# Moving two token blocks' transfers and splits to other places, and one block product to another bank, in an encoder block on one core

## The chip, the cores and the metric

The kernel runs on one core of one Trainium2 chip. The metric is the device time of one execution in microseconds (us); lower is better. Each kernel is run several times and the median is given, with the lowest and the highest beside it. A profiled execution also gives a span: the time from the first to the last instruction in the trace. It is a little shorter than the execution's own time.

## The reference, cut to what matters

The kernel computes one encoder block in float32 with a batch of 1, 1024 tokens and a width of 1024. Three mixers run side by side on the same normalised input, each is gated and projected, the three are merged by sigmoid gates, and one output projection follows:

```python
h = rms_norm(x, g_pre[layer])
a_qkv, bq, bk, bv, mq, ga, gb, gm, mg = jnp.split(h @ w_in[layer], split_at, axis=-1)
...                                   # oa: dilated windows, ob: grouped queries, om: cross-attention
ya = (oa * jax.nn.silu(ga)) @ w_br_a[layer]
yb = (ob * jax.nn.silu(gb)) @ w_br_b[layer]
ym = (om * jax.nn.silu(gm)) @ w_br_m[layer]
gates = jax.nn.sigmoid((mg + b_merge[layer]).astype(jnp.float32)).astype(dt).reshape(b, s, N_BRANCHES, d)
merged = gates[:, :, 0] * ya + gates[:, :, 1] * yb + gates[:, :, 2] * ym
out = merged @ w_out[layer]
x = x + rms_norm(out, g_post[layer])
```

The change touches how the last part of `mg` is computed. `mg` has 3 x 1024 columns, that is 24 *units* of 128 columns. A unit is one product of a 1024 x 128 block of weights with the 1024 x 1024 input. In the kernel the rows of the result are the 128 columns of the weights, and the 1024 tokens run along the free axis.

## The kernel before, in words

**Numbers.** TensorE (PE) multiplies float32 values in three passes. Each operand is split into a high part, rounded to a shorter type (fp32r), and a low part, the rest. A product is then high x high + high x low + low x high. The helper `split` (lines 103 to 106) makes the two parts: ScalarE (ACT) copies the source into the high tile (line 105), then VectorE (DVE) subtracts the high part from the source and writes the low tile (line 106). The helper `passes` (lines 121 to 125) issues the matmuls of one product into one bank of the accumulator memory (PSUM). The input lies in SBUF as `hh0` to `hh7` (high) and `hl0` to `hl7` (low), each 128 x 1024, one for each block of 128 input channels.

**Banks.** PSUM has eight banks of 128 x 512. Two of them belong to the dense units for the whole kernel: `psd` (lines 61 and 62), which hands out a tile named `d`, two in turn. The other six are laid out anew for each stage by `phase_psum` (line 67). In the stage of the pairs they are a ring of six single banks (`pss1`, tiles named `s`), and in the stage of the branch projections three tiles of two banks each (`pss`, tiles named `sc`).

**Stages.** In order of time: the memory branch and the keys of the grouped-query branch, woven into dense units; the grouped-query attention; two stages of block products for values and keys; the dilated attention (twelve items, four groups of heads by three dilations), woven into the last dense units (`weave`, line 176); the *pairs*; the branch projections; the output projection. PE's instructions stand in the order in which the program writes them in the whole kernel. In the dilated stage and in the pairs that order is also kept on ACT, DVE, GpSimd (POOL) and SyncE (SP), because a `manual_schedule` covers these engines there (lines 1601 and 1647). An instruction there never overtakes one that is written ahead of it on its engine. SP issues nearly all transfers from one queue, in order; a transfer whose target is still being read holds up all those behind it.

**The pairs** (lines 1642 to 1822). Two of the 24 units are computed earlier, and the other 22 form eleven pairs, n = 0 to 10. A pair is a product of two weight units (256 columns) with 1024 channels by 1024 tokens, seen as a 2 x 2 by 2 x 2 block matrix and computed by Winograd's scheme with seven block products in place of eight (`PRODUCTS`, line 1656): A11·B11, A12·B21, S2·T2, S3·T3, S4·B22, S1·T1, A22·T4. A is the weights, B the input, S1 to S4 are sums of weight blocks, and T1 to T4 sums of token blocks. One block product has 12 matmuls of 128 x 128 by 128 x 512 and fills one bank. In the last pair the order is another (`nth`, line 1675): A22·T4 is fifth, S4·B22 sixth and S1·T1 seventh.

The token sums T1 to T4 are computed once, early in the kernel, and lie in DRAM (`tsd`). Each consists of four tiles of 128 x 512, loaded raw by `load_block` (line 1584) into the low tile and then split in place by `split_block` (line 1589). T2 and T3 are loaded and split while the last item of the dilated attention runs. Of T1, tiles 0 and 1 are loaded there too (line 1463), and tiles 2 and 3 at the head of the pairs (line 1811). T4 goes into the upper token halves of `hh0` to `hh3` and `hl0` to `hl3` (line 1653), which nothing reads in the pairs but which the dense units read until the end of the dilated stage. It is loaded last of all (line 1813).

For each pair and each i from 0 to 6 the main loop (lines 1815 to 1822) writes the block product on PE (`prod`), the evacuation of the product before it (`evac`), and a *slot* of work for later (`slot`, line 1759):

- `evac` adds on DVE: intermediate results into tiles `sp` (line 1689), results into tiles `rs` (line 1689), which are then multiplied by the token's reciprocal norm `rb` (line 1695). ACT applies tanh to `rs` (line 1696) and sends it to DRAM.
- `block_of` splits a weight block or a weight sum (`sf`) into a tile `ch` of high and low halves (lines 105 and 106).
- `own_blocks` splits A11 and A12 of the next pair into `wh` and `wl`, 128 x 1024 each.
- `weight_sum` (line 1666) makes S1 to S4 on POOL from the weights `wr`. `load_pair` (line 1571) loads these, two tiles in turn.
- In pair 0 the slots 2, 3 and 4 also split T1 (two tiles each in slots 2 and 3) and T4 (all four in slot 4). In pairs 0 to 4 some slots hold a step of the dilated attention's last combination (`COM`).

After the pairs come 24 units of the branch projections (`y_unit`, two times 12 matmuls into one `sc` tile) with weights loaded into `wr` and split into halves of `wh` (`y_split`).

Of the kernel before, what the change touches and what calls it, by code (L numbers as in the profile page):

```python
# [9 lines left out]
R = mybir.dt.float32r  # L10
# [5 lines left out]
S = 1024  # L16
NT = 8
P = 128
# [32 lines left out]
def block(ctx: ExitStack, tc: tile.TileContext, x, xT, memT, cst, msk, bcst, tabA, gpost,  # L51
# [10 lines left out]
    def psd():  # L62
        return ps.tile([P, 512], F32, name="d", tag="d", bufs=2)
# [15 lines left out]
    def pss1():  # L79
        return bank["p"].tile([P, 512], F32, name="s1", tag="s1", bufs=bank["n"][1])  # L80
# [41 lines left out]
    def passes(out_ps, terms):  # L122
        n = len(terms)
        for i, (a, b) in enumerate(terms):
            PE.matmul(out_ps, a, b, start=i == 0, stop=i == n - 1)  # L125
# [117 lines left out]
    def pool(name, side="left"):  # L243
        p = tc.tile_pool(name=name, bufs=1, side=side, reuse_waits="tile")
        return p, p.__enter__()

    def close(p):
        p.__exit__(None, None, None)
# [605 lines left out]
    def slot():  # L854
        return vp.tile([P, 1024], R, name="sl", bufs=8)
# [257 lines left out]
    tbp, tb = pool("tb")  # L1113
    tab = [tb.tile([P, S], F32, name=f"tab{j}") for j in range(2)]
# [8 lines left out]
    for n in range(6):  # L1123
        for i, (an, bn) in enumerate(PRODUCTS):
            dst = pss1()
# [54 lines left out]
    with tc.tile_pool(name="aa", bufs=1, reuse_waits="tile") as aa:  # L1180
# [263 lines left out]
        def joined(*pieces):  # L1444
            pieces = [x for x in pieces if x]
            return (lambda: [fn() for fn, _ in pieces]), JOINED

        def plan(it, pre, nxt):

            out = []  # L1450

            def combining(T):
                while todo and T == STEP_T[-len(todo)]:
                    todo.pop(0)()

            def tokens(T):
                if T >= 2:
                    for nm, k in late[:2]:
                        split_block(nm, k)
                    del late[:2]  # L1460
                if T == 5:
                    token_tiles("T1", [ab.tile([P, S], R, name=f"a{c}", bufs=2) for c in "qk"])
                    load_block("T1", (0, 1))

            def keys(key, T):
                (k_fetch if T == 1 else k_add)(*key)

            def ready():
                if pre and pre["key"][1] == 2:
                    fetch, *steps = combine(pre["key"][0], [OG.pop((pre["key"][0], x)) for x in range(3)])  # L1470
                    fetch()
                    todo.extend(steps)

            if it and not pre:
                out.append(it["scores"][0])
            for T in range(NT if it else 4):
                if T == 2 and pre:
                    out.append(pre["stats"])
                if T < LAG:
                    if pre:  # L1480
                        out.append(pre["trans"][T + 8 - LAG])
                elif it:
                    out.append(it["trans"][T - LAG])
                if it:
                    out.append(it["soft"][T])
                out.append((lambda T=T: combining(T), 0.0))
                if it and not nxt:
                    out.append((lambda T=T: tokens(T), 0.0))
                if it and it["ahead"] and T in (1, 5):
                    out.append((lambda T=T: keys(it["ahead"], T), 0.0))  # L1490
                if T == 3:
                    out.append(joined(pre and pre["pv"][1], it and it["scores"][1]))
                    if it:
                        out.append(it["values"][1])
                    if pre and it:
                        out.append((ready, 0.0))
                if T == 7:
                    out.append(joined(it["pv"][0], nxt and nxt["scores"][0]))
                    if nxt:
                        out.append(nxt["values"][0])  # L1500
            return out
# [67 lines left out]
        def load_pair(n, u):  # L1569
            BL[n][u] = wp.tile([P, 1024], F32, name="wr", bufs=WR)  # L1570
            nc.sync.dma_start(BL[n][u], wu[U_M + pairs[n][u]])

        def own_blocks(n):
            wh = wp.tile([P, 1024], R, name="wh")
            wl = wp.tile([P, 1024], R, name="wl")
            split(wh, wl, BL[n][0])
            for j in range(2):
                BL[n][("A11", "A12")[j]] = wh[:, half[j]], wl[:, half[j]]
# [3 lines left out]
        def token_tiles(nm, tiles):  # L1582
            TB.setdefault(nm, []).extend([t[:, half[x]] for x in range(2)] for t in tiles)

        def load_block(nm, ks=range(4)):
            for k in ks:
                nc.sync.dma_start(TB[nm][k][1].bitcast(F32), tsd[int(nm[1]) - 1, k])

        def split_block(nm, k):
            h, l = TB[nm][k]  # L1590
            split(h, l, l.bitcast(F32))
# [26 lines left out]
        for n in range(len(seq)):  # L1618
# [5 lines left out]
            last = n + 1 == len(seq)  # L1624
# [24 lines left out]
    lo, hi = half  # L1649
    srp, sr = pool("sr")  # L1650
    SF = [sr.tile([P, 512], F32, name=f"sf{j}") for j in range(4)]
    token_tiles("T1", [tb.tile([P, S], R, name=f"T1{k}", tag=f"tab{k - 2}") for k in (2, 3)])
    TB["T4"] = [(hh[k][:, hi], hl[k][:, hi]) for k in range(4)]
    TB["B11"] = [(hh[k][:, lo], hl[k][:, lo]) for k in range(4)]
    TB["B21"] = [(hh[k + 4][:, lo], hl[k + 4][:, lo]) for k in range(4)]
# [2 lines left out]
    last = len(pairs) - 1  # L1658

    def part(n, j):  # L1660
        return BL[n][j // 2][:, half[j % 2]]

    def weight_sum(n, j):
        u, v, op = {1: (part(n, 2), part(n, 3), OP.add), 2: (SF[0], part(n, 0), OP.subtract),
                    3: (part(n, 0), part(n, 2), OP.subtract), 4: (part(n, 1), SF[1], OP.subtract)}[j]
        G.tensor_tensor(SF[j - 1], u, v, op=op)  # L1666

    def block_of(n, nm):
        src = part(n, 3) if nm == "A22" else SF[int(nm[1]) - 1]
        t = sr.tile([P, 2, 512], R, name="ch", bufs=5)  # L1670
        split(t[:, 0], t[:, 1], src)
        BL[n][nm] = t[:, 0], t[:, 1]

    def nth(n, i):

        return PRODUCTS[{4: 6, 5: 4, 6: 5}.get(i, i) if n == last else i]

    def prod(n, i):
        an, bn = nth(n, i)
        dst = pss1()  # L1680
        ah, al = [v.rearrange("p (k f) -> p k f", k=4) for v in BL[n][an]]
        passes(dst, [t for k in range(4) for t in (
            (ah[:, k], TB[bn][k][0]), (ah[:, k], TB[bn][k][1]), (al[:, k], TB[bn][k][0]))])
        return dst
# [46 lines left out]
    def g_mult(i, k):  # L1731
        if i != 1:
            ot, gt = GG[i, k]
            V.scalar_tensor_tensor(ot, ot, 0.5, gt, op0=OP.mult, op1=OP.mult)
# [24 lines left out]
    def slot(n, i):  # L1759

        first = n == 0
        if not first and i == 1 and n < last:
            load_pair(n + 1, 1)
        if i == 6 and n + 1 < last:
            load_pair(n + 2, 0)
        todo_ = (("S2",), ("S3", "A22"), ("S4",), ("S1",)) if first else (("A22",), ("S4",), ("S1",))
        for nm in todo_[i] if i < len(todo_) else ():
            block_of(n, nm)
        if first:
            for nm, k in {2: (("T1", 0), ("T1", 1)), 3: (("T1", 2), ("T1", 3)), 4: (("T4", 0), ("T4", 1), ("T4", 2), ("T4", 3))}.get(i, ()):  # L1770
                split_block(nm, k)
        if n < last:
            if i == 3:
                weight_sum(n + 1, 1)
                weight_sum(n + 1, 3)
                own_blocks(n + 1)
            elif i == 4:
                weight_sum(n + 1, 2)
                block_of(n + 1, "S3")
            elif i == 5:  # L1780
                weight_sum(n + 1, 4)
                block_of(n + 1, "S2")
        if (n, i) in COM:
            com[COM[n, i]]()
        if (n, i) == (5, 0):
            close(cbp)
            pre["pp"], pre["p"] = pool("pre", "right")
        k = n - (last - 4)
        if 0 <= k < 4:
            if i == 0:  # L1790
                g_load(2, k)
            elif i == 4:
                g_mult(2, k)
        if n == last:
            if i == 0:
                y_load(0)
                y_load(1)
            elif i in (3, 4):
                for k in range(2 * i - 6, 2 * i - 4):
                    g_split(2, k, lo)  # L1800
            elif i in (5, 6):
                for k in range(2 * i - 10, 2 * i - 8):
                    g_split(2, k, hi)
            if i == 2:
                y_split(0)
                y_load(2)

    for j in (1, 2, 3, 4):
        weight_sum(0, j)
    load_pair(1, 0)  # L1810
    load_block("T1", (2, 3))
    load_pair(1, 1)
    load_block("T4")
    before = None
    for n in range(len(pairs)):
        for i in range(7):
# [276 lines left out]
```

## Time and profile before

| what | value |
|---|---|
| time before, median of 3 runs | 1434.83 us (1433.94 to 1435.69) |
| profiled execution, its own time | 1434.1 us |
| span of that execution | 1432.3 us |
| PE busy | 1405.2 us (98% of the span) |
| PE's weight loads (PEld) busy | 1130.6 us (79%) |
| DVE busy | 993.7 us (69%) |
| ACT busy | 657.0 us (46%) |
| POOL busy | 509.9 us (36%) |
| granted TensorE clock, mean | 0.999 of full speed |
| HBM traffic over the span | 138 GB/s |

How to read the rows that follow. Times are in us from the start of the span. The page names an engine, a line of the kernel (L125 is line 125), an operation and the tiles that it writes and reads (`sc<-hh,wh` writes `sc` and reads `hh` and `wh`). In a timeline a row begins with its start and its duration; `x4` stands for four like instructions in a row, and a bracket gives the idle time just ahead of it on its engine and what ended that. The idle time of an engine that does not set the pace costs nothing. Matmuls are pipelined, so the durations of single matmuls overlap, and the distance between starts is the better measure. In the chain of waits the work that ended last is followed back to what released each step. SPq is SP's queue of transfers.

### The profile page before, as it was taken

The numbers are of one execution on the slowest core, as the hardware profiler recorded it, in microseconds if no ns is written. First come the engines' busy times: TensorE is split into PE (matmuls) and PEld (weight loads), VectorE is DVE, ScalarE is ACT, GpSimd is POOL, SyncE is SP. The second block draws the span as 40 slices with busy tenths as digits, with TensorE's granted clock in tenths as the row PEclk, the third lists the DMA queues.
The fourth block names the chain that finished last, engine by engine and source line by source line (L and its number), as shares of the span: only waits on it lengthen the run. The fifth ranks groups of instructions, "written<-read, shape, count | busy, mean of one in ns | idle before, by whom it ended". The sixth has DMA issues, their size and how long they took to land.

```text
span 1432.3 us, 21216 instructions
## 1 busy us (share of the span) xinstructions
PE 1405.2 (98%) x7556; PEld 1130.6 (79%) x7556; DVE 993.7 (69%) x1765; ACT 657.0 (46%) x1423; POOL 509.9 (36%) x390
## 2 busy tenths in 40 slices
PE   7999999999999999999999999999999999999998
PEld 7899986666666888888888878877787887888887
DVE  7765468777773785688776778755887787659643
ACT  6543356665555445322156666656433434213221
POOL 0415603666675001333143354411343330044222
PEclk9999999999999999999999999999999999999999
DMA  6332012222210879444553445364334454667122
GB/s 233 109 120 75 16 64 76 88 97 75 75 55 31 281 241 299 139 175 155 189 149 110 119 137 157 89 176 140 129 122 147 177 176 151 245 220 276 42 88 103
DMA packets 114138, 198.68 MB, mean 139 GB/s; under 512 B 24624, under 2 KB 55408, under 8 KB 114032
## 3 DMA queue, kind: packets, MB, share of 16 engines
q1 hardware_dynamic: 87824, 166.75, 36.4%
q10 hardware_dynamic: 26208, 30.58, 6.1%
q8 instruction: 59, 0.97, 0.3%
q14 instruction: 47, 0.39, 0.1%
HBM read 142.40 MB, written 54.89 MB: 138 GB/s over the span
## 4 chain that ended last, share of the span: by engine, by line
PE 82%; DVE 6%; ACT 4%; DMA 3%; issue 3%; POOL 2%; SPq 0%; ACTq 0%; POOLq 0%; DVEq 0%
PE s L125 19%; PE sc L125 9%; PE d L143 7%; PE d L147 6%; PE d L145 6%; PE s L1059 5%; PE sc L1939 5%; PE ov L761 4%; PE s L1343 2%; PE tr L1399 2%; PE s L745 2%; PE tr L727 2%; PE s L746 2%; PE d L542 2%; PE d L1059 1%
## 5 line engine op out<-in xcount | busy, mean ns | idle before, releaser
L143 PE MATMUL d<-hh,wh 128*128 128x512 f32 x480 | 194.8, 406 | 1.7 <-DVE fth L228 1.7
L145 PE MATMUL d<-hl,wh 128*128 128x512 f32 x480 | 194.4, 405 | 0.0
L147 PE MATMUL d<-hh,wl 128*128 128x512 f32 x480 | 190.5, 397 | 0.0
L752 POOL TENSOR_TENSOR bl<-bl,bp 128x512 f32<-128x512 f32 x96 | 131.4, 1369 | 53.6 <-ACT bp L748 48.1
L105 ACT ACTIVATE wh<-wr 128x512 fp32r<-128x512 f32 (+1 forms) x91 | 69.6, 772 | 141.9 <-PE sc L125 78.4
L125 PE MATMUL sc<-hh,wh 128*128 128x512 f32 x384 | 118.3, 389 | 2.2 <-ACT rs L1696 2.2
L106 DVE TENSOR_TENSOR wl<-wr,wh 128x512 fp32r<-128x512 f32 (+1 forms) x63 | 74.3, 1192 | 57.8 <-ACT wh L105 57.6
L143 PEld LDWEIGHTS d<-hh,wh 128*128 128x128 f32 x480 | 90.3, 188 | 25.7 <-issue 5.2
L147 PEld LDWEIGHTS d<-hh,wl 128*128 128x128 f32 x480 | 90.5, 189 | 21.3 <-issue 4.5
L145 PEld LDWEIGHTS d<-hl,wh 128*128 128x128 f32 x480 | 90.5, 189 | 20.8 <-issue 6.3
L1356 ACT ACTIVATE pra<-pra,sts 128x192 f32<-128x192 f32 (+2 forms) x192 | 84.4, 442 | 46.2 <-DVE sts L1355 45.6
L728 DVE TENSOR_REDUCE bn<-tr 128x1 f32<-128x512 f32 x128 | 86.0, 685 | 17.5 <-PE tr L727 16.2
L748 ACT ACTIVATE bp<-s 128x512 f32<-128x512 f32 x128 | 75.9, 595 | 46.7 <-PE s L746 45.6
L106 DVE TENSOR_TENSOR ch<-sf,ch 128x512 fp32r<-128x512 f32 x68 | 57.7, 850 | 45.3 <-ACT ch L105 45.3
L1666 POOL TENSOR_TENSOR sf<-wr 128x512 f32<-128x512 f32 x22 | 33.8, 1556 | 149.2 <-DMA wr<-in_wu 65.8
L125 PEld LDWEIGHTS sc<-hh,wh 128*128 128x128 f32 x384 | 72.1, 188 | 17.5 <-issue 2.6
L105 ACT ACTIVATE ch<-sf 128x512 fp32r<-128x512 f32 x68 | 41.5, 627 | 90.6 <-PE s L125 46.4
L1207 DVE SCALAR_TENSOR_TENSOR t2a<-d,tab 32x512 f32<-32x512 f32 x96 | 66.0, 687 | 22.2 <-PE d L147 20.5
L1870 POOL TENSOR_TENSOR acc<-acc,th 128x1024 f32<-128x1024 f32 x15 | 40.6, 2707 | 111.7 <-DVE th L1869 111.7
L997 POOL TENSOR_TENSOR sf<-wr 128x512 f32<-128x512 f32 x12 | 18.9, 1574 | 166.9 <-DMA wr<-in_wu 109.3
L125 PE MATMUL sc<-hl,wh 128*128 128x512 f32 x192 | 74.7, 389 | 0.0
L125 PE MATMUL s<-hh,ch 128*128 128x512 f32 x224 | 73.7, 390 | 0.8 <-ACT ch L105 0.8
(392 smaller groups left out, 3733.4 us busy)
## 6 DMA issues: line engine op xcount, KB each, us to landing
wr<-in_wu SPq DMA_DIRECT2D x64, 512.0 KB
kd<-kr ACTq DMA_DIRECT2D x48, 256.0 KB
th<-thd SPq DMA_DIRECT2D x24, 512.0 KB
thd<-rs ACTq DMA_DIRECT2D x44, 256.0 KB
g2d<-fth SPq DMA_DIRECT2D x24, 256.0 KB
kraw<-kd SPq DMA_DIRECT2D x12, 512.0 KB
kswp<-kd SPq DMA_DIRECT2D x48, 128.0 KB
wgt<-wgd SPq DMA_DIRECT2D x24, 256.0 KB
```

Of the source, the lines that this page charges most:

```text
L105: A.activation(dst_h, src, AF.Copy)
L106: V.tensor_tensor(dst_l, src, dst_h.bitcast(F32), op=OP.subtract)
L125: PE.matmul(out_ps, a, b, start=i == 0, stop=i == n - 1)
L143: PE.matmul(dst, wh[:, k, :], hh[k][:, t], start=k == 0, stop=False)
L145: PE.matmul(dst, wh[:, k, :], hl[k][:, t], start=False, stop=False)
L147: PE.matmul(dst, wl[:, k, :], hh[k][:, t], start=False, stop=k == 7)
L728: fp["last"] = V.tensor_reduce(st[i]["n"][:, j, c:c + 1], s, axis=AX.X, op=OP.min)
L748: A.activation(pp, s, AF.Exp, scale=-1.0)
L752: G.tensor_tensor(lsum[i % 2], lsum[i % 2], pp, op=OP.add)
L1059: PE.matmul(now[j], a, b, start=k == 0 and q == 0, stop=k == end and q == 2)
L1356: A.activation(src, src, AF.Exp, scale=-1.0, bias=bias, accum_out=sts[:, h, 1, T:T + 1])
L1939: PE.matmul(parts[h], *terms[h][j], start=j == 0, stop=j == 23)
```

## The change

Three things are edited. All four tiles of T1 are loaded at the same point of the dilated stage where two were loaded before, so the two tiles of the tab buffers are handed out there too. At the head of the pairs T4's loads stand first, ahead of the two weight loads of pair 1, and T1's second half is gone from there. In pair 0 the slots that split T1 and T4 are 1, 2 and 3 where they were 2, 3 and 4. Last, the last block product of the last pair takes a bank of the dense units (`psd`) where it took one of the ring of six (`pss1`). The matmuls, splits and transfers are the same in number and size.

```diff
                 if T == 5:
                     token_tiles("T1", [ab.tile([P, S], R, name=f"a{c}", bufs=2) for c in "qk"])
-                    load_block("T1", (0, 1))
+                    token_tiles("T1", [tb.tile([P, S], R, name=f"T1{k}", tag=f"tab{k - 2}") for k in (2, 3)])
+                    load_block("T1")
...
     SF = [sr.tile([P, 512], F32, name=f"sf{j}") for j in range(4)]
-    token_tiles("T1", [tb.tile([P, S], R, name=f"T1{k}", tag=f"tab{k - 2}") for k in (2, 3)])
     TB["T4"] = [(hh[k][:, hi], hl[k][:, hi]) for k in range(4)]
...
     def prod(n, i):
         an, bn = nth(n, i)
-        dst = pss1()
+        dst = psd() if (n, i) == (last, 6) else pss1()
...
         if first:
-            for nm, k in {2: (("T1", 0), ("T1", 1)), 3: (("T1", 2), ("T1", 3)), 4: (("T4", 0), ("T4", 1), ("T4", 2), ("T4", 3))}.get(i, ()):
+            for nm, k in {1: (("T1", 0), ("T1", 1)), 2: (("T1", 2), ("T1", 3)), 3: (("T4", 0), ("T4", 1), ("T4", 2), ("T4", 3))}.get(i, ()):
                 split_block(nm, k)
...
     for j in (1, 2, 3, 4):
         weight_sum(0, j)
+    load_block("T4")
     load_pair(1, 0)
-    load_block("T1", (2, 3))
     load_pair(1, 1)
-    load_block("T4")
```

## The prediction

> **What bounds the kernel now.** I read the page first (busy shares, then the chain of waits), then what TensorE (PE) itself waited for, stretch by stretch, and then the timeline of each engine around those waits.
>
> ```profile
> span 1432.3 us, 21216 instructions
> ...
> PE 82%; DVE 6%; ACT 4%; DMA 3%; issue 3%; POOL 2%; SPq 0%; ACTq 0%; POOLq 0%; DVEq 0%
> ```
> ```profile
> 1014.00:1101.00 87.00, 86.89 (x384) 71.58 (x382) 68.52 (x88) 32.80 (x50) 30.44 (x18) 1.00 0.41 129
> 1101.00:1205.00 104.00, 103.28 (x454) 85.24 (x455) 82.03 (x107) 44.48 (x69) 31.93 (x20) 1.00 0.44 156
> ...
> 1208.00:1339.00 131.00, 131.00 (x579) 108.44 (x580) 92.77 (x74) 32.40 (x49) 40.61 (x15) 1.00 0.63 226
> ```
>
> The second fence is the view by stretches: stretch, its length, then the busy time of PE, of its weight loads, of DVE, ACT and POOL, the granted clock, the share of the DMA engines, GB/s. PE is busy nearly all the time at full clock, so a change that leaves the matmuls alone can only win where PE stands idle. In the part that the change touches (pairs of dense units, then the branch projections) PE was stopped at three places. They are these, in PE's timeline (start, duration, and in brackets the idle time before it and its releaser):
>
> ```profile
> 1005.61 0.84 PE L125 MATMUL s<-aq,ch 128*128 128x512 f32 x3
> ...
> 1008.33 0.39 PE L125 MATMUL s<-hh,ch 128*128 128x512 f32 x1
> ...
> 1011.39 0.51 PE L125 MATMUL s<-hl,ch 128*128 128x512 f32 x1 [0.73 <-DVE hl L106]
> ...
> 1013.08 0.50 PE L125 MATMUL s<-hl,ch 128*128 128x512 f32 x1 [0.72 <-DVE hl L106]
> ...
> 1013.65 0.40 PE L125 MATMUL s<-hh,wh 128*128 128x512 f32 x1
> ```
> ```profile
> 1101.72 0.50 PE L125 MATMUL s<-hh,ch 128*128 128x512 f32 x1 [0.84 <-ACT ch L105]
> ```
> ```profile
> 1202.77 0.84 PE L125 MATMUL s<-aq,ch 128*128 128x512 f32 x3
> ...
> 1207.85 0.47 PE L125 MATMUL sc<-hh,wh 128*128 128x512 f32 x1 [2.20 <-ACT rs L1696]
> ```
>
> A block product is 12 matmuls. Undisturbed it takes 1008.33 - 1005.61 = 2.72 us (0.227 a matmul). Place A is pair 0's last product, with token block T4: 1013.65 - 1008.33 = 5.32, so 2.60 too long, waiting for DVE's low parts of T4. Place B, in pair 5, costs 0.84. Place C is the step to the first branch projection: the last product would end at 1202.77 + 2.72 = 1205.49, and the next matmul starts at 1207.85, which is 2.36 later; with the slower first matmul after a stop I take 2.4.
>
> **The change part by part.** No matmul, split or transfer is added or removed.
>
> *The bank (place C).* The first projection's tile takes two banks that the ring of six held; one of them held the last product. That product goes to one of the two banks of the dense units, which nothing has used since pair 0 began. PE then waits for nothing at 1205.49. Late next would be the second projection's weights, split behind the last three results:
>
> ```profile
> 1209.60 0.63 ACT L105 ACTIVATE wh<-wr 128x512 fp32r<-128x512 f32 x1 [0.40 <-ACT rs L1696]
> ```
> ```profile
> 1210.26 0.69 DVE L106 TENSOR_TENSOR wh<-wr,wh 128x512 fp32r<-128x512 f32 x1 [1.83 <-ACT wh L105]
> ```
>
> They are ready at 1210.23 (high) and 1210.95 (low). The second projection starts at 1205.49 + 24 x 0.227 = 1210.94 and reads the low part two matmuls later, 1211.39. That fits with 0.4 to spare. Worth 2.4; between 0 (transfers of the projections bound PE: their stretch above has a DMA share of 0.63 and no PE idle) and 2.4.
>
> *T1's second half, loaded in the dilated stage.* Two issues of about 0.4 us each join SP's queue behind this one, in a stage where SP waits on its own:
>
> ```profile
> 975.25 1.25 SPq L1587 DMA_DIRECT2D ak<-tsd  x1
> ...
> 996.38 0.36 SPq L1571 DMA_DIRECT2D wr<-in_wu  x1
> ...
> 998.35 0.38 SPq L1571 DMA_DIRECT2D wr<-in_wu  x1
> 998.83 3.20 SPq L1587 DMA_DIRECT2D hl<-tsd  x4
> ```
>
> Behind them stand only a gate store, T4's loads, and small statistics stores. I cost it at nothing; at most 1 us, if that store's buffer were waited for.
>
> *T4's loads first.* They overwrite hl0 to hl3, so they wait for the last dense unit's reads of those tiles, the first and the last here:
>
> ```profile
> 982.83 0.39 PE L145 MATMUL d<-hl,wh 128*128 128x512 f32 x1
> ...
> 984.89 0.39 PE L145 MATMUL d<-hl,wh 128*128 128x512 f32 x1
> ```
>
> So they go out at 983.2 to 985.3 in place of 998.83 to 1002.03. SP stands still behind them until 985.3; what waits there is one gate store and the last statistics stores, and the first that needs a buffer back from that gate store is the evacuation that DVE starts at 997.65 (below). I cost the wait at nothing. In the old order the data was awaited:
>
> ```profile
> 1006.02 0.64 ACT L105 ACTIVATE hh<-hl 128x512 fp32r<-128x512 f32 x1 [1.04 <-DMA hl<-tsd]
> ...
> 1008.19 1.29 ACT L105 ACTIVATE hh<-hl 128x512 fp32r<-128x512 f32 x2 [0.52 <-DMA hl<-tsd]
> ```
>
> 1008.19 - 998.83 is at most 9.4 us from first issue to last landing; from 983.2 that gives 992.6, long before use. The two weight loads `wr` of pair 1 then share the queues with six loads fewer (T1's two, T4's four), so they land no later than before.
>
> *The splits, sooner.* On DVE the low parts of T1 and T4 move ahead. Steps of DVE, from where the order differs:
>
> ```profile
> 996.82 0.68 DVE L106 TENSOR_TENSOR ch<-wr,ch 128x512 fp32r<-128x512 f32 x1
> 997.65 0.69 DVE L1689 TENSOR_TENSOR rs<-s,sp 128x512 f32<-128x512 f32 x1
> 998.37 0.69 DVE L1695 TENSOR_TENSOR rs<-rs,rb 128x512 f32<-128x512 f32 x1
> 998.98 0.68 DVE L106 TENSOR_TENSOR ch<-sf,ch 128x512 fp32r<-128x512 f32 x1
> ...
> 1005.01 1.23 DVE L106 TENSOR_TENSOR wl<-wr,wh 128x1024 fp32r<-128x1024 f32 x1 [0.26 <-ACT wh L105]
> ...
> 1006.76 6.27 DVE L106 TENSOR_TENSOR hl<-hl,hh 128x512 fp32r<-128x512 f32 x4
> ...
> 1014.75 0.68 DVE L1689 TENSOR_TENSOR rs<-s,sp 128x512 f32<-128x512 f32 x1
> ...
> 1019.37 0.69 DVE L106 TENSOR_TENSOR ch<-wr,ch 128x512 fp32r<-128x512 f32 x1 [0.56 <-ACT ch L105]
> ```
>
> One step costs 0.60 to 0.72. After 996.82 come T1's first two (997.42, 998.02), rs (998.62), its scaling (999.34), S4 (999.95), T1's other two (1000.55, 1001.15), an evacuation (1001.76), S1 (1002.36) and T4's first at 1002.96, against 1006.76. Meanwhile POOL does pair 1's four weight sums, and both engines slow each other:
>
> ```profile
> 1005.46 3.63 POOL L1666 TENSOR_TENSOR sf<-wr 128x512 f32<-128x512 f32 x2 [9.11 <-DMA wr<-in_wu]
> ```
> ```profile
> L106 DVE TENSOR_TENSOR hl<-hl,hh x4: 1185/1768/1776, 1006.8 to 1011.3; 128x512 fp32r<-128x512 f32 x4
> ```
> ```profile
> L1666 POOL TENSOR_TENSOR sf<-wr x7: 1287/1297/2278, 993.4 to 1044.9; 128x512 f32<-128x512 f32 x7
> L106 DVE TENSOR_TENSOR wl<-wr,wh x3: 1226/1261/2053, 1005.0 to 1044.8; 128x1024 fp32r<-128x1024 f32 x3
> ```
>
> (The last three: ns, least, median, most.) The sums began at 1005.46 because a `wr` landed then; that load now lands no later, and S1's split lets go of the first sum's tile at 1003.1, so they start between 1003.1 and 1005.46. I take 1003.1, the harder case for DVE. Four T4 splits at the worst 1.77 end at 1010.0; PE needs the last at 1008.33 + 10 x 0.227 = 1010.6. So place A vanishes and PE enters pair 1 at 1011.05, 2.60 earlier. Pair 1's `wl` now stands behind T4: first T4 split 0.6, three at the interval of 1.69 seen between the T4 stops above (1013.08 - 1011.39), then 2.05: it ends at 1010.7; PE reads it at 1011.5. No stop, 0.6 us at worst (1010.0 + 2.05).
>
> *What is late next: place B.* DVE and ACT run behind PE through pairs 1 to 5 and set their own pace:
>
> ```profile
> L1689 DVE TENSOR_TENSOR rs<-s,sp 128x512 f32<-128x512 f32 x42 | 28.6, 682 | 0.6 <-PE s L125 0.6
> ...
> L1689 DVE TENSOR_TENSOR sp<-s,sp 128x512 f32<-128x512 f32 x31 | 21.1, 680 | 0.0
> ```
> ```profile
> DVE ch L106 <- ACT ch L105: 12.3, 11, 2.5
> ...
> ACT rs L1696 <- DVE rs L1695: 35.9, 14, 6.6
> ```
> ```profile
> 1099.54 0.69 DVE L106 TENSOR_TENSOR ch<-wr,ch 128x512 fp32r<-128x512 f32 x1 [0.55 <-ACT ch L105]
> ```
>
> The first rows cover 1013 to 1206: 73 evacuations waited 0.6 us for PE in all. The second are the waits of DVE and ACT from 1014 to 1101: on each other, never on PE. From 1019.37 to 1099.54 the same split comes round four times in 80.17 us, 20.0 a pair, where PE needs 7 x 2.72 = 19.04. The loop loses ground until PE stops at 1101.72. So PE's 2.60 does not count there; what counts is by how much the loop starts earlier, d. Old: rs at 1014.75. New: behind `wl` come four steps of 0.60, so 1010.7 + 2.4 = 1013.1: d = 1.7. Bounds: all at the slowest rows, 1010.0 + 2.05 + 2.4 = 1014.5, d = 0.3; without slowing, the loop gains more than 2.60 + 0.84 = 3.4 and place B vanishes, which caps the worth. I take 1.7, since the interval comes from the same four splits beside the same four sums. B's stop grows from 0.84 to 1.7.
>
> Sum: 2.4 + 1.7 = 4.1. The profiled execution took 1434.1 (span 1432.3), so 1430.0 for it; the median of the runs shown, 1434.83, is 0.73 above, so the forecast is 1434.83 - 4.1 = 1430.7. What a measurement can tell from no change is 0.2%, 2.9 us.
>
> **The rivals.**
> (1) Place B doesn't grow: the slowing is small, d is 2.6 to 3.4, gain 5.0 to 5.8: 1429.0 to 1429.8. For it: should POOL start as late as 1005.46, T4's splits are through by then, at 0.60 each. Against: the same sums slowed the same splits to 1.77.
> (2) Full blocking: DVE's splits and POOL's sums take strict turns. Four splits (2.4), `wl` (1.2) and four sums at 1.29 (5.2) make 8.8 from 1002.96: 1011.8, then 2.4: 1014.2, d = 0.6, 1431.8; with d = 0.3, 1432.1. Against: in the old order the same work took less, from 1005.01 to about 1013. The Trainium skill, page "SBUF — State Buffer", section "Who interferes with whom", states such a lock for a DVE instruction with two SBUF inputs beside a GpSimd one that reads SBUF: the second blocks for the whole instruction; the trace agrees, with 1768 ns beside POOL against the 0.69 us of the split at 1019.37.
> (3) Place C isn't won: the projections' transfers, asked for no earlier, bound PE. Gain 1.7: 1433.1. For it: DMA share 0.63 there. Against: PE never idles in that stretch.
> (4) Slower: T4's loads stay stuck in SP's queue, and T4's four splits now stand ahead of `wl` on DVE. If the last of T4 lands at L, `wl` ends by L + 0.64 (ACT) + 1.77 + 2.05 = L + 4.5. PE reads it 0.45 into pair 1's first product, which now starts at 1013.65, so that product slips by L + 4.0 - 1013.65. Against C's gain of 2.4, slower by 2.9 needs a slip of 5.3: L above 1014.9, more than 30 us after the first issue, where the rows have 9.4. At that point: 1437.7.
>
> **How the numbers follow.** Forecast (d from 1.0 to 2.6, 1429.8 to 1431.4) 0.58; rival 1 0.13; rival 2 0.15; rival 3 0.10; rival 4 0.04. Rival 1 ends at 1429.0, rivals 2 and 3 at 1433.1; the runs shown lie up to 0.9 either side of their median, of which I add 0.5 below and the whole above: 1428.5 to 1434.0. Rival 4 and as much again for what I have overlooked stay outside. Faster by over 2.9 (below 1431.9): 0.58 + 0.13 + half of rival 2 = 0.78, less 0.06 of the forecast's upper end (1431.4), which that scatter can carry over the line, 0.72; within: the other half of rival 2, rival 3 and those 0.06, with little taken off for slower, 0.23; slower: 0.05.
>
> **What would show it.** Right: T4's issues at 983 to 986; no stop of PE between 1008 and 1014, the first product of pair 1 at about 1011; the rs that stood at 1014.75 at about 1013; a stop near 1100 of 1.7 us, on the same split; `sc` directly behind the last product, its stop gone. Wrong: `wl` the releaser of a stop near 1011; a stop at B of more than 2.6 (then d is below 0.84); stops among the projections; T4's data awaited again.

## The result, and the profile after

The changed kernel takes 1430.15 us (median of 5 runs, 1428.24 to 1431.53). The kernel before, run beside it, takes 1434.83 us (5 runs, 1433.94 to 1437.1). The ratio is 0.9963, with a 95% interval from 0.9949 to 0.9978. So it is faster by 4.7 us, or 0.37%. The forecast was 1430.7, a gain of 4.1. One execution of the kernel before, among the 21 that were run beside `e8` to `e10` below, took 2228.95 us at a mean clock of 0.588 and is left out of every figure here.

The profiled execution of the changed kernel took 1431.53 us. Its span and the first line of its chain of waits:

```profile
span 1429.7 us, 21221 instructions
...
PE 76%; DVE 8%; ACT 5%; issue 4%; DMA 3%; POOL 3%; SPq 1%; ACTq 0%; POOLq 0%; DVEq 0%
```

PE's share of the chain fell from 82% to 76%, and DVE, ACT and POOL gained. The chain now runs for some time through the loop that leads to the one long stop that is left; besides DVE, ACT and POOL, two loads of `wr` stand in it (shown under place B at the end). The view of waits for PE, from the last part of the dilated stage to the end, first of the kernel before and then of the changed one (releaser, us in all, times, longest):

```profile
PE sc L125 <- ACT rs L1696: 2.2, 1, 2.2
PE s L125 <- DVE hl L106: 1.8, 3, 0.7
PE s L125 <- ACT ch L105: 0.8, 1, 0.8
```
```profile
PE s L125 <- ACT ch L105: 1.6, 1, 1.6
```

Place A (the T4 product) and place C (ahead of the projections) are gone. Place B (pair 5's S4 product) has nearly doubled. The same three places in PE's timeline of the changed kernel:

```profile
1008.33 1.52 PE L125 MATMUL s<-T,ch 128*128 128x512 f32 x6
1009.69 0.39 PE L125 MATMUL s<-hh,ch 128*128 128x512 f32 x1
...
1012.41 0.39 PE L125 MATMUL s<-hh,wh 128*128 128x512 f32 x1
...
1099.22 0.84 PE L125 MATMUL s<-ak,ch 128*128 128x512 f32 x3
1101.62 0.50 PE L125 MATMUL s<-hh,ch 128*128 128x512 f32 x1 [1.56 <-ACT ch L105]
...
1204.03 1.52 PE L125 MATMUL d<-T,ch 128*128 128x512 f32 x6
1205.39 0.39 PE L125 MATMUL sc<-hh,wh 128*128 128x512 f32 x1
```

At A the T4 product lasts from 1009.69 to 1012.41, which is its undisturbed 2.72. At C the last product writes a tile `d`, and the first projection follows after 6 x 0.227 = 1.36: no gap. At B, by starts, three matmuls from 1099.22 end at 1099.90, and PE goes on at 1101.62, so the stop is 1.72 long. In the kernel before it was 1101.72 - (1100.05 + 0.68) = 0.99. The view of waits leaves out the shortest idle times, and one short stop is not seen in it: pair 4's S4 product took from 1080.43 to 1083.58 in this profile, 0.4 longer than 2.72.

The transfers (queue of SP), and what DVE, ACT and POOL did with T4:

```profile
977.73 0.90 SPq L1588 DMA_DIRECT2D T<-tsd  x2
...
984.56 2.38 SPq L1588 DMA_DIRECT2D hl<-tsd  x4
...
997.70 1.49 SPq L1572 DMA_DIRECT2D wr<-in_wu  x2
```
```profile
1003.06 2.18 ACT L105 ACTIVATE hh<-hl 128x512 fp32r<-128x512 f32 x4
```
```profile
1004.28 5.79 DVE L106 TENSOR_TENSOR hl<-hl,hh 128x512 fp32r<-128x512 f32 x4
1009.99 2.31 DVE L106 TENSOR_TENSOR wl<-wr,wh 128x1024 fp32r<-128x1024 f32 x1
...
1014.63 0.68 DVE L1689 TENSOR_TENSOR rs<-s,sp 128x512 f32<-128x512 f32 x1
```
```profile
1004.44 3.38 POOL L1666 TENSOR_TENSOR sf<-wr 128x512 f32<-128x512 f32 x2 [6.77 <-DVE ch L106]
```

T4 goes out at 984.56, and ACT copies its four high parts in one run without a wait. DVE's four T4 splits take 5.79 us beside POOL's sums, and `wl` 2.31 behind them.

Times counted from the start of the profile can mislead here. This execution started its pairs 1.31 us later than that of the kernel before (993.19 against 991.88). All of that lies ahead of the first moved instruction: set against the same matmuls of the kernel before, it loses 1.2 us near 825 and 0.55 near 890, and gains 0.3 near 945. The profile of `e1_bank` below shows the same two losses (1.0 and 0.7 us), and its instructions there are those of the kernel before; the second profile of the changed kernel has 0.3 and 0.4. So they belong to the execution. From here on, times count from the first block product of the pairs.

### The profile page after: what moved, and what is told of

Its sections match the earlier page's. It is cut to its first block, busy times and chain, and to the rows that moved or that the text cites. A ratio compares the mean times of both kernels' runs of the same rounds, so it can differ in the third digit from the quotient of the medians.

```text
span 1429.7 us, 21221 instructions
## 1 busy us (share of the span) xinstructions
PE 1404.9 (98%) x7556; PEld 1130.7 (79%) x7556; DVE 996.6 (70%) x1765; ACT 655.9 (46%) x1423; POOL 508.9 (36%) x390
## 4 chain that ended last, share of the span: by engine, by line
PE 76%; DVE 8%; ACT 5%; issue 4%; DMA 3%; POOL 3%; SPq 1%; ACTq 0%; POOLq 0%; DVEq 0%
PE s L125 16%; PE sc L125 9%; PE d L143 6%; PE d L147 6%; PE d L145 6%; PE s L1059 5%; PE sc L1938 5%; PE ov L761 4%; PE s L1343 2%; PE tr L1399 2%; PE s L745 2%; PE tr L727 2%; PE s L746 2%; PE d L542 2%; PE d L1059 1%
## 5 line engine op out<-in xcount | busy, mean ns | idle before, releaser
L106 DVE TENSOR_TENSOR wl<-wr,wh 128x512 fp32r<-128x512 f32 (+1 forms) x63 | 78.7, 1262 | 57.9 <-ACT wh L105 57.7
L1211 POOL TENSOR_TENSOR aq<-t1a,t2a 128x512 f32<-128x512 f32 x24 | 46.2, 1929 | 82.9 <-DVE t1a L1210 82.7
```

What stands on the lines that cost most here:

```text
L106: V.tensor_tensor(dst_l, src, dst_h.bitcast(F32), op=OP.subtract)
```

## The experiments

Each kernel was timed against the kernel before on the same chip. The kernel before took 1434.98 us there for `e1` to `e4`, 1435.38 for `c_after` and `e5` to `e7`, and 1435.40 for `e8` to `e10`. The table has the time, the ratio to the kernel before, and four distances of the profiled execution. *Pair 1*: the start of pair 1's first product, which is late when PE stops at A. *rs*: the start of DVE's first `rs` after `wl`, the point by which the prediction measured how early the loop starts. *B*: the start of pair 5's S4 product behind its stop. *End*: the start of the first projection. All four count from the first block product. *Rest* is from the first projection to the end of the span.

| kernel | us, median (range) | ratio (95%) | pair 1 | rs | B | end | rest |
|---|---|---|---|---|---|---|---|
| before | see above | 1 | 21.77 | 22.87 | 109.84 | 215.97 | 224.45 |
| changed, first profile | 1430.15 (1428.24 to 1431.53) | 0.9963 (0.9949 to 0.9978) | 19.22 | 21.44 | 108.43 | 212.20 | 224.31 |
| `c_after`: the changed kernel | 1430.26 (1429.96 to 1431.94) | 0.9967 (0.9954 to 0.9979) | 19.17 | 21.41 | 107.61 | 211.40 | 224.41 |
| `e1_bank` | 1431.68 (1429.2 to 1433.35) | 0.9979 (0.9969 to 0.9988) | 21.72 | 22.73 | 109.26 | 213.03 | 224.40 |
| `e2_moves` | 1433.98 (1431.23 to 1436.34) | 0.9990 (0.9981 to 0.9999) | 19.22 | 20.54 | 107.23 | 213.38 | 226.13 |
| `e3_loads` | 1428.76 (1428.37 to 1430.43) | 0.9960 (0.9947 to 0.9972) | 19.96 | 21.06 | 107.88 | 211.65 | 224.11 |
| `e4_slots` | 1432.96 (1432.21 to 1434.51) | 0.9987 (0.9978 to 0.9995) | 20.78 | 23.61 | 110.66 | 214.44 | 224.35 |
| `e5_s4` | 1427.58 (1426.94 to 1427.89) | 0.9945 (0.9933 to 0.9958) | 19.21 | 21.42 | no stop | 210.00 | 224.34 |
| `e6_s4_before` | 1431.08 (1428.96 to 1431.82) | 0.9968 (0.9957 to 0.9980) | 21.01 | 22.11 | no stop | 211.43 | 224.35 |
| `e7_sums` | 1427.76 (1427.47 to 1429.26) | 0.9949 (0.9935 to 0.9962) | 19.17 | 19.42 | 106.77 | 210.55 | 224.05 |
| `e8_fill` | 1434.18 (1432.3 to 1436.8) | 0.9993 (0.9983 to 1.0003) | 21.19 | 22.28 | 108.50 | 214.66 | 224.48 |
| `e9_both` | 1426.74 (1426.1 to 1429.68) | 0.9951 (0.9937 to 0.9965) | 19.19 | 19.44 | no stop | 209.59 | 224.08 |
| `e10_s4_ring` | 1431.42 (1429.56 to 1432.78) | 0.9976 (0.9967 to 0.9985) | 19.17 | 21.42 | no stop | 212.21 | 226.02 |

Where there is a stop at B, B minus rs is 86.97, 86.99, 86.20, 86.53, 86.69, 86.82, 87.05, 87.35 and 86.22 in the order of the table. (The stop of `e8_fill` is a short one, 0.26 by starts.) Pair 1 starts anywhere from 19.17 to 21.77, and B doesn't follow it. B follows rs, as the prediction's loop says.

### The bank alone

```diff
-        dst = pss1()
+        dst = psd() if (n, i) == (last, 6) else pss1()
```

> The kernel before with the bank change alone. My theory: only the stop of PE ahead of the first branch projection goes (2.4 us by starts, 2.20 in its bracket); the stops at pair 0's T4 product (2.60 by starts, 1.8 in brackets) and at pair 5's S4 product (0.84) stay. Gain 2.4 us, near 1432.4. Rival (the projections are bound by their transfers): the time comes back as stops among the projections, gain near 0.

The ratio gives a gain of 1.7 to 4.4 us, with 3.3 between the medians; I had expected 2.4. Waits of PE in the pairs in this profile:

```profile
PE s L125 <- DVE hl L106: 1.7, 3, 0.7
...
PE s L125 <- ACT ch L105: 0.3, 1, 0.3
```

C is gone, and A and B stay. The rest after the first projection (224.40) is that of the kernel before (224.45), so the rival with transfers that bind the projections falls. The end of the pairs comes 2.94 sooner: C's 2.36, and 0.58 because B happened to come sooner (109.26 against 109.84).

### The moves alone

The changed kernel with `dst = pss1()` as before.

> The changed kernel with the last product back in the ring of six, so the transfers and splits alone are moved. My theory: the stop at the T4 product goes (2.60), but PE then stops longer at pair 5's S4 product (1.5 to 1.7 in place of 0.84), and the stop ahead of the projections stays at 2.2; gain 1.7 us, near 1433.1. Rival: the stop at S4 doesn't grow, gain 2.6 or more (1432.2 or less). Other rival (DVE and POOL take strict turns): the gain is 0.6 or less.

The interval of the ratio allows 0.1 to 2.7 us, and the medians are 1.0 apart (I had expected 1.7), so the time alone tells little. In the profile the end of the pairs comes 2.59 sooner, and the rest is 1.7 longer than in the kernel before, which has the same stop at C. Two things are to be seen in it. First, T4's splits beside the sums, DVE and POOL:

```profile
1004.78 2.50 DVE L106 TENSOR_TENSOR hl<-hl,hh 128x512 fp32r<-128x512 f32 x4
```
```profile
1004.95 5.85 POOL L1666 TENSOR_TENSOR sf<-wr 128x512 f32<-128x512 f32 x2 [6.77 <-DVE ch L106]
```

In this execution the splits ran at 0.6 each and POOL was held up (5.85 for its first two sums, where the changed kernel shows 3.38). The loop started 0.9 sooner than in the changed kernel, and the stop at B was 0.81, no longer than before. That is rival 1 in one execution (its d is 2.33, just under the 2.6 to 3.4 that the rival gave). Second, the view by stretches right behind the stop at C (the number behind POOL's count is the granted clock):

```profile
1207.00:1209.00 2.00, 1.93 (x5) 1.59 (x6) 0.65 (x1) 0.99 (x3) 0.00 (x0) 0.53 0.91 352
1209.00:1211.00 2.00, 2.00 (x7) 1.57 (x6) 0.69 (x1) 0.44 (x1) 0.00 (x0) 0.61 0.37 135
```

PE ran at little more than half speed for some 4 us after the stop. `e8_fill` and `e10_s4_ring` follow this up.

### Loads or slots

`e3_loads` is the changed kernel with the old slots of the splits. `e4_slots` is the kernel before with the new slots and the new bank, but the loads in their old places.

```diff
-            for nm, k in {1: (("T1", 0), ("T1", 1)), 2: (("T1", 2), ("T1", 3)), 3: (("T4", 0), ("T4", 1), ("T4", 2), ("T4", 3))}.get(i, ()):
+            for nm, k in {2: (("T1", 0), ("T1", 1)), 3: (("T1", 2), ("T1", 3)), 4: (("T4", 0), ("T4", 1), ("T4", 2), ("T4", 3))}.get(i, ()):
```

> The changed kernel with the splits of T1 and T4 back in the old slots (T1 in 2 and 3, T4 in 4); loads early, bank changed. My theory: T4's data no longer has to be awaited, but wl of pair 1 and its weight sums again stand ahead of T4's splits, so PE still stops 1 to 2 us at the T4 product. DVE has the same work in the same time, so its first rs of pair 0's tail starts as in the changed kernel (about 1014.6) and the stop at pair 5's S4 is shorter by what PE lost before: the time is that of the changed kernel within 0.5 us (1430.2). Rival (what counts is how soon PE gets T4): slower than the changed kernel by the 1 to 2 us of that stop.

> The kernel before with the sooner splits and the bank change, and with the loads of T1's second half and of T4 where they stood before. My theory: T4's data lands at 1006 to 1008.2 as before, the splits ahead of wl wait for it, wl of pair 1 ends near 1012.6, and PE stops about 1 us at pair 1's first product with wl as the releaser; DVE's first rs starts near 1015.0, no earlier than before (1014.75), so the move of the splits alone is worth nothing or costs 0.3: gain over the kernel before 2.1 to 2.4, all of it the bank's. Rival (the place of the splits is what matters, not the loads): gain 4 or more, like the changed kernel.

PE in `e3_loads`, then in `e4_slots`:

```profile
1011.43 0.50 PE L125 MATMUL s<-hl,ch 128*128 128x512 f32 x1 [0.51 <-DVE hl L106]
...
1099.92 0.50 PE L125 MATMUL s<-hh,ch 128*128 128x512 f32 x1 [0.70 <-ACT ch L105]
```
```profile
1010.54 0.50 PE L125 MATMUL s<-hl,ch 128*128 128x512 f32 x1 [0.33 <-DVE hl L106]
...
1012.22 0.50 PE L125 MATMUL s<-hl,ch 128*128 128x512 f32 x1 [0.71 <-DVE hl L106]
...
1102.67 0.50 PE L125 MATMUL s<-hh,ch 128*128 128x512 f32 x1 [1.76 <-ACT ch L105]
```

With the loads early and the splits in the old slots, PE stops at A for 0.5 (I expected 1 to 2) and reaches pair 1 about 0.75 later than in the changed kernel. That costs nothing: rs and B are among the earliest of the kernels with POOL's sums, and the time is that of the changed kernel (0.9960 against 0.9963 and 0.9967). With the splits early and the loads late, rs comes 0.74 *later* than in the kernel before, and B 0.82 later, although PE enters pair 1 1.0 sooner. So the early loads carry the whole gain of the moves, and sooner splits without them cost 0.8 in the profile (I had expected 0 to 0.3, and the releaser of PE's stop was T4's low parts, not `wl`).

### Place B

`c_after` is the changed kernel once more. `e5_s4` moves the split of the next pair's S4 ahead, to slot 6 of the pair before. `e6_s4_before` makes the same edit to the kernel before with the new bank, and so without the moves of T1 and T4.

```diff
-        todo_ = (("S2",), ("S3", "A22"), ("S4",), ("S1",)) if first else (("A22",), ("S4",), ("S1",))
+        todo_ = (("S2",), ("S3", "A22"), ("S4",), ("S1",)) if first else (("A22",), (), ("S1",))
...
                 block_of(n + 1, "S2")
+            elif i == 6:
+                block_of(n + 1, "S4")
```

> The changed kernel once more, beside the three that follow: 1430.2 us, stop at pair 5's S4 product 1.5 to 1.7 us, no other stop from the pairs on. It also gives a second profile, in which the stretch before the pairs shows whether the 1.3 us that the first profile lost near 815 us, where both kernels have the same instructions, belong to the kernel or to that one execution: by the first, again about 1.3 late there against the kernel before; by the second, not.

> The changed kernel with the split of S4 of the next pair moved from slot 1 to slot 6 of the pair before, ahead of the last two tanh steps and of A22's split. My theory: the stop at pair 5's S4 product is set only by the place of that split in the orders of ACT and DVE; it is then ready about 3 us sooner and the stop vanishes: 1.6 us faster than the changed kernel, 1428.6. Rival: DVE and ACT are behind with everything, so the stop moves to another wait of the pairs (S1's block, a bank of the ring, or wl) and the time stays at 1430.2.

> The kernel before with the bank change and with S4's split in slot 6, so without the moves of T1 and T4. My theory: the stop at pair 5 is gone here too, and the stop at pair 0's T4 product (2.60) counts in full: 2.6 us slower than the kernel with all three (near 1431.2), where with the stop at pair 5 in place the moves are worth 1.7. Rival (the moves are worth the same 1.7 or less whatever is at pair 5): the distance to the kernel with all three is 1.7 or less.

PE at B in `c_after`, and the same place in `e5_s4`:

```profile
1100.30 0.50 PE L125 MATMUL s<-hh,ch 128*128 128x512 f32 x1 [1.24 <-ACT ch L105]
```
```profile
1096.33 0.84 PE L125 MATMUL s<-ak,ch 128*128 128x512 f32 x3
1097.01 0.39 PE L125 MATMUL s<-hh,ch 128*128 128x512 f32 x1
...
1099.73 1.20 PE L125 MATMUL s<-aq,ch 128*128 128x512 f32 x3
1100.77 0.86 PE L125 MATMUL s<-ak,ch 128*128 128x512 f32 x3
```

In `c_after` the stop is 1.24 by its bracket, where I had expected 1.5 to 1.7. In `e5_s4` the S4 product follows at 3 x 0.227 = 0.68 with no stop. A small wait takes its place, too short for the view of waits: the first three matmuls of the next product, S1·T1, take 1100.77 - 1099.73 = 1.04 in place of 0.68, because the third reads the low part of S1, which DVE writes until 1100.38. So 0.36 of the stop moved on to S1's block; by the rival all of it would have. The end of the pairs comes at 210.00, where 77 products of 2.72 make 209.4. That is 1.40 before `c_after` and 2.20 before the first profile of the changed kernel. The medians are 2.7 apart, which is more than I expected (1.6). The two profiled executions are 3.3 apart, and 1.9 of that lies ahead of the pairs, which started at 992.69 in the one and at 990.76 in the other; why that start moves by up to 3 us between executions (990.63 to 993.69 over all of them) stays open.

In `e6_s4_before` the stop at A is there:

```profile
1011.68 0.50 PE L125 MATMUL s<-hl,ch 128*128 128x512 f32 x1 [0.56 <-DVE hl L106]
...
1013.37 0.50 PE L125 MATMUL s<-hl,ch 128*128 128x512 f32 x1 [0.73 <-DVE hl L106]
```

It is 3.5 us slower than `e5_s4` by the medians. By the profiles it is 1.80 later at pair 1 and 1.43 at the end of the pairs; its stop at A was shorter than usual (pair 1 at 21.01, not 21.77), and `e5_s4` loses 0.36 at S1's block, which this one doesn't. The expected 2.6 lies between the two, and these runs do not settle whether the moves are worth more without B than the 1.4 to 2.2 that they bring with it.

### Pair 1's weight sums on DVE

```diff
-        G.tensor_tensor(SF[j - 1], u, v, op=op)
+        (V if n == 1 else G).tensor_tensor(SF[j - 1], u, v, op=op)
```

> The changed kernel with the four weight sums of pair 1 on DVE in place of POOL. My theory: POOL's sums slow DVE's splits beside them; without them T4's four splits take 2.4 us (5.79 now) and wl 1.2 (2.31 now), while DVE gets four sums of 0.6: the first rs of pair 0's tail starts near 1012.5 (relative to the same start of the pairs as in the profile of the changed kernel) in place of 1014.63, and the stop at pair 5 falls from 1.6 to near 0: 1.6 us faster than the changed kernel. Rival (the slow splits have another cause, DMA traffic say): the splits keep 1.45 each, DVE gets 2.4 more, the stop at pair 5 grows by 2.4: slower by 2.4.

T4's four splits, in the changed kernel and then here (least, median and most, in ns):

```profile
L106 DVE TENSOR_TENSOR hl<-hl,hh x4: 686/1777/1792, 1004.3 to 1008.3; 128x512 fp32r<-128x512 f32 x4
```
```profile
L106 DVE TENSOR_TENSOR hl<-hl,hh x4: 687/689/692, 1003.6 to 1005.4; 128x512 fp32r<-128x512 f32 x4
```

Without POOL's sums beside them all four take 0.69. DVE does four instructions more and is still 2.0 us sooner at rs (19.42 against 21.41). The stop at B is 0.40 in place of 1.24, and the kernel is faster than `c_after` by 2.5 between the medians; by the end of the pairs it is 0.85 (I had expected 1.6). So POOL's sums are what slows the splits. The Trainium skill states on the page "SBUF — State Buffer", section "Who interferes with whom", that the order of issue decides which of the two is blocked. The traces agree that either can be: the splits in the changed kernel, the sums in `e2_moves`. That the order decides it they don't show: in both, DVE's first split starts ahead of POOL's first sum, by 0.16 and 0.17 us.

### The stop at C and the clock

`e8_fill` gives PE ten matmuls to do in the stop at C of the kernel before. `e10_s4_ring` is `e5_s4` with the last product back in the ring. `e9_both` joins `e5_s4` and `e7_sums`.

```diff
             before = (n, i, ps_)
+    fill = psd()
+    an, bn = nth(last, 6)
+    ah, al = [q.rearrange("p (k f) -> p k f", k=4) for q in BL[last][an]]
+    passes(fill, [t for k in range(4) for t in (
+        (ah[:, k], TB[bn][k][0]), (ah[:, k], TB[bn][k][1]), (al[:, k], TB[bn][k][0]))][:10])
     evac(*before)()
```

> The kernel before with ten extra matmuls, whose result nothing reads, between the last block product and the first branch projection: PE works through 10 x 0.227 = 2.27 us of the 2.36 us in which it stands still there, and nothing else is moved. My theory after the first seven runs: the stop costs more than its own length, because in about a third of the executions the granted clock falls to 0.53 to 0.61 for some 4 us after it (mean clock of the execution 0.997 or less); with the stop filled the mean clock is 0.998 or more in all but a few executions, and the median is 0.3 to 0.8 us below the kernel before, while the first projection starts at the same time as before relative to the pairs. Rival (the lower clock in some executions has nothing to do with the stop): 0.997 or less in about a third of the executions as before, and the same median.

> The changed kernel with both further edits: S4's split in slot 6 of the pair before, and pair 1's four weight sums on DVE. My theory: PE has no stop left in the pairs with the first alone (210.0 us from the first block product to the first projection, where 77 products of 2.72 make 209.4), so the second adds nothing: 1427.6, as with the first alone, within 0.5. Rival: both gains add, 1426 or less.

> The changed kernel with S4's split in slot 6 and with the last product back in the ring of six: the bank's worth with no stop of PE in the pairs. My theory: PE reaches the end of the pairs 1.2 to 1.6 us sooner than in the changed kernel, but DVE's last evacuations, which release the ring, don't wait for PE alone; the stop ahead of the projections is 2.2 by its bracket as before and the time is 2.4 to 3.2 above the kernel with the bank (1430.0 to 1430.8), with a mean clock of 0.997 or less in about a third of the executions. Rival: the clock is 0.999 in all of them and the distance is 2.4 or less.

The stretches behind place C, of `e8_fill` (filled) and of `e10_s4_ring` (PE stands still until 1203.58):

```profile
1205.00:1207.00 2.00, 2.00 (x9) 1.42 (x8) 1.56 (x3) 1.09 (x2) 0.00 (x0) 1.00 0.15 18
1207.00:1209.00 2.00, 2.00 (x10) 1.64 (x9) 0.58 (x1) 0.99 (x2) 0.00 (x0) 1.00 0.87 195
```
```profile
1205.00:1207.00 2.00, 2.00 (x6) 1.52 (x6) 0.69 (x1) 0.63 (x1) 0.00 (x0) 0.50 0.50 190
1207.00:1209.00 2.00, 2.00 (x8) 1.58 (x7) 0.00 (x0) 0.00 (x0) 0.00 (x0) 0.69 0.52 180
```

The mean clocks of the single executions tell more. The mean was 0.997 or less in 22 of 78 executions of kernels in which PE stands still at C (17 of 56 of the kernel before, 3 of 11 of `e2_moves`, 2 of 11 of `e10_s4_ring`, where I had expected a third). It was so in 2 of 68 executions of kernels in which it doesn't; the 11 of `e8_fill` are among these 68, and none of them was so low. The line at 0.997 is not sharp: the profiled execution of `e10_s4_ring`, which shows the fall, has a mean of 0.998, and so has that of `e8_fill`, which shows none. A mean of 0.998 or less stands in 43 of the 78 and in 9 of the 68. In the two profiles that show the fall (`e2_moves` and `e10_s4_ring`), the rest is 226.13 and 226.02, against a median of 224.35 in the others: it costs about 1.7 us where it happens. Averaged over all executions with the stop that is, as an estimate, 0.5 (22/78 x 1.7) to at most 0.9 (43/78 x 1.7).

The median of `e8_fill` is 1.2 below the kernel before, but its interval reaches from 0.9983 to 1.0003, so a gain in time from filling the stop is not shown. Its first projection starts 1.31 sooner after the start of the pairs, but that comes from shorter stops at A and B in this profile. What is shown is that the low clock comes with the stop.

`e10_s4_ring` is 3.9 slower than `e5_s4` from the start of the pairs to the end of the span: 2.21 to the first projection and 1.68 behind it. I had 2.4 to 3.2. By the ratios the distance is 4.4. `e9_both` ends its pairs at 209.59, 0.4 before `e5_s4`, and 0.9951 against 0.9945 is no difference: the 0.36 at S1's block is gone there, and the times show no further gain from freeing DVE. `e5_s4` and `e9_both` are both faster than the changed kernel: 0.9945 (0.9933 to 0.9958) and 0.9951 (0.9937 to 0.9965) of the time before.

## Why the prediction was right

**Place C.** Forecast: 2.4, with the second projection's weights ready 0.4 before they are needed. Right: no gap, the rest unchanged (`e1_bank`), 2.36 in the profile. The weights' high and low parts were ready at 1210.13 and 1210.85, and PE needed the low part at 1211.28, again 0.4 later. What it lacked is the clock after the stop, by the estimate above worth 0.5 to 0.9 on average. In the profile of the kernel before, the clock behind the stop was 1.00, so that one execution could not show it. This term was too small, then: 2.4 where 2.9 to 3.3 belongs. The other term was a little too large (1.7 for d, where 1.43 and 1.46 were measured). The measured gain is known only to 3.2 to 7.3 us, so the difference between the 4.1 forecast and the 4.7 and 5.1 between the medians of the two series needs no cause, and it is the profiles, not the time, that confirm the terms. From the start of the pairs to the first projection the two profiles of the changed kernel gain 3.77 and 4.57.

**T4's loads.** Forecast: out at 983.2 to 985.3, no wait for them. Measured 984.56 to 986.94, in an execution that ran 1.31 later. Right, and T1's two loads 6 us ahead of them cost nothing that can be seen. Rival 4 fell: ACT's four copies stand without a wait.

**The splits, place A.** Forecast: A vanishes, pair 1 starts 2.60 sooner. Measured 2.55. The four splits with `wl` were to take 5.7 and 2.05, and took 5.79 and 2.31. But I put the gain down to the splits standing sooner together with the loads. `e3_loads` shows that the loads suffice, and `e4_slots` that the sooner splits alone make the loop start later. So that step of the account was wrong. The sum did not suffer from it, because it went by d, the start of the loop, and not by PE's 2.60.

**Place B.** Forecast: it grows from 0.84 to 1.7, and the moves are worth d = 1.7. Measured: 1.56 and 1.24 by the brackets, d = 1.43 and 1.46, B sooner by 1.41 and 2.23. The size is less sure than it looks, since nine profiles hold B only within 86.2 to 87.4 of rs, a scatter of 1.2. That the place was S4's split is shown by `e5_s4`: with that split sooner, 0.36 of the stop is left, at the next product.

What the prediction had wrong here is what the loop consists of. It took DVE and ACT to wait only on each other. The view of waits that it read, of the kernel before from 1014 to 1101, also has these lines:

```profile
POOL sf L1666 <- DMA wr<-in_wu: 23.4, 2, 13.0
...
ACT ch L105 <- POOL sf L1666: 11.1, 7, 3.7
```

ACT's splits wait for POOL's weight sums, and those for a load. In the changed kernel the chain of waits that ends at B runs that way in two of the pairs, here the second (start, us, what):

```profile
1078.24 0.71 DVE ch L106
1078.96 5.16 DMA wr<-in_wu
...
1084.25 3.53 POOL sf L1666 x2
1087.81 0.64 ACT ch L105
```

DVE's split of A22 is the last to read `wr`; the next load of `wr` goes out right behind it, POOL's sums wait for its landing, and ACT's split of a sum waits for them. The other pass is the same (a load of 4.78 us from 1039.01). So two loads and four sums are part of the loop too, some 17 us of the 87 from rs to B. That B moves with the start of the loop holds all the same; whether a sooner load would shorten the loop was not tried.

**Rivals 1 and 2.** Whether DVE or POOL is held up decides between rival 1 and the forecast. Five profiles with T4's splits in the new slots beside POOL's sums and early loads show four times 5.78 or 5.79 for the splits (both of the changed kernel, `e5_s4`, `e10_s4_ring`) and once 2.50 (`e2_moves`). What decides it is not shown: in all five DVE's first split starts 0.16 to 0.17 us before POOL's first sum. Rival 2's strict turns (8.8 us for the splits, `wl` and the sums, d = 0.6) did not show: in the changed kernel all of it was done 8.0 us after T4's first split began (1009.99 + 2.31 - 1004.28), and d was 1.43.

## What to carry to other kernels

When a wait on one engine is taken away, ask for the next place where that engine waits, and what sets the time of that place; the gain is what that chain gains, not what the first engine does. Test such a place with the smallest edit of order that goes round it: here one split moved ahead of two tanh steps took away nearly all of the stop that had absorbed part of the gain. And when a transfer is late, move the transfer before moving its consumer: a consumer that stands sooner in an in-order queue holds up all that is behind it.

## What the hardware showed that I had not expected

A stop of PE of 2.2 us by its bracket (2.36 by starts) was followed in two of three profiles that have it by some 4 us at a granted clock of 0.5 to 0.7, which costs 1.7 us more than the stop itself. By the mean clocks this befell between about a quarter and about half of the executions with the stop (22 of 78 at 0.997 or less, 43 of 78 at 0.998 or less); with PE kept busy through the same stretch, none of 11 executions had a mean of 0.997 or less. The Trainium skill, page "TensorE: Matmul & The Clock Gate", section "Why this matters for your kernels", warns of idle gaps above about 3 us; here a shorter one sufficed now and then.

Two engines that slow each other can do so either way where the code of that stage is the same: 5.79 and 3.38 us (DVE's four splits, POOL's two sums) in one execution, 2.50 and 5.85 in another.
